# Softmax probabilities normalised on GpSimd instead of on VectorE and ScalarE

## The chip, the cores and the metric

The kernel runs on one core of a Trainium2 chip. The core has a matrix engine (TensorE, in the profile PE, its weight loads PEld), VectorE (DVE), ScalarE (ACT), GpSimd (POOL) and a queue that issues transfers (SyncE, SP). The engines run beside each other, each through its own list of instructions in order, and wait for each other by semaphores. The metric is the device time of one execution in microseconds; the time before is the median of three runs.

## The reference

One inference step of a two-layer trunk for 128 context tokens and 512 latent tokens that share the weights. Every layer projects its normalised input, runs a gated convolution, grouped-query attention and a state-space scan beside each other, adds up the three gated branches, and ends in a SwiGLU. What matters here is attention, for 16 query heads over 4 key heads of 64 channels; a latent block of 128 queries sees 512 latent and 128 cached keys:

```python
s = jnp.einsum('bqkrd,bskd->bkrqs', qi, k).astype(jnp.float32)
p = jax.nn.softmax(s, axis=-1).astype(v.dtype)
return jnp.einsum('bkrqs,bskd->bqkrd', p, v)
```

## The kernel before

All 640 tokens go through a layer together. A matrix product takes its weights and its activations as pairs of high and low halves, three products each, accumulated in PSUM. Weights come in through SP, ACT makes the high half (tile `wh`) and DVE the low half.

Attention works in tiles of 128 queries of one head against 640 keys, 64 such tiles a layer, and after every 16 a smaller one for the context tokens of four heads. A tile goes through these steps, each a generator of its own: `attn_scores` (line 1271) multiplies q by k on PE and takes the row extreme on DVE (into `mx`); `attn_exp` (line 1254) exponentiates on ACT from PSUM into a tile `c` and gets the row sums; `attn_norm` (line 1236) takes the reciprocal of the sums on DVE and multiplies the tile by it, in place; `attn_turn` (line 1308) transposes it on PE by five products with the identity (`bps<-ident,c`); `attn_split` makes a high half (ACT) and a low half (DVE) of the transposed tile, in `pt`; `attn_out` multiplies by V on PE (`bps<-pt,c`) and adds up the result.

The order of the instructions is not written out. A planner in the program does it: it keeps a clock for each engine (class `Clock`), every recorded instruction adds a cost to it (lines 133 to 163; all instructions are recorded at line 132, and so the profile shows that line), and `pump` (line 538) lets the generator step next that can start first by these clocks, as long as that is no later than what the main thread could do. The main thread, `layer` (line 1895), issues the projections: during attention these are the q projections, the gates (`gates`), the GLU of the scan branch and its output branch. Then comes `drain(att)` (line 1946), which steps attention alone until it is finished, and the projection of attention's output after it. In the planner's clock a norm on DVE costs 70 + 640 / 1.6 = 470, one on ACT 100 + 640 / 1.2 = 633; a dependence between engines adds a hop of 100.

Before the change, `attn_norm` picks the engine whose clock is behind (line 1243). POOL issues transfers only: those of the FFN weights that are added to what is in `pt`.

Of the kernel before, what the change touches and what calls it, by code (L numbers as in the profile page):

```python
# [10 lines left out]
AF = mybir.ActivationFunctionType  # L11
OP = mybir.AluOpType
# [100 lines left out]
class Engine:  # L113
# [5 lines left out]
    def __getattr__(self, op):  # L119
        f, key, clock = getattr(self.eng, op), self.key, self.clock  # L120

        def is_ap(x):
            return hasattr(x, "partition_size")

        def size(x):
            n = 1
            for d in x.shape[1:]:
                n *= d
            return n

        def call(*args, **kw):
            res = f(*args, **kw)  # L132
            out = kw.get("out", args[0] if args else None)
            ins = [x for x in list(args[1:] if "out" not in kw else args) +
                   [v for k, v in kw.items() if k not in ("out", "accum_out")] if is_ap(x)]
            outs = [out.name] + ([kw["accum_out"].name] if "accum_out" in kw else [])
            n = max([size(out)] + [size(x) for x in ins]) if key != "pe" else size(out)
            if key == "pe":
                if op == "transpose":
                    cost = 2 * n / 2.4  # L140
                elif ins[-1].dtype == F32R:
                    cost = max(n, 256) / 2.4
                else:
                    cost = 4 * n / 2.4
                    if out.shape[0] == 32:
                        cost /= 3
            elif key == "act":
                cost = 100 + n / 1.2 + (90 if "accum_out" in kw else 0)
            elif key == "dve":
                one = op in ("tensor_scalar", "tensor_copy", "memset") and all(x.space == out.space for x in ins)  # L150
                cost = 70 + n / (1.6 if one else 0.96)
            else:
                s = max([clock.t["pe"] if key == "dma" else clock.t[key]] + [clock.avail.get(x, 0.0) for x in outs] +
                        [clock.w.get(x.name, 0.0) for x in ins])
                if key == "pool":
                    clock.t[key] = e = s + 1000
                else:
                    clock.issue = max(clock.issue, s) + 475.0
                    rate = 180.0 if min(x.shape[-1] for x in [out] + ins) < 128 else 360.0
                    clock.t[key] = e = max(clock.t[key], clock.issue) + 4 * n * out.shape[0] / rate  # L160
                for x in outs:
                    clock.w[x], clock.by[x] = e + (4000 if key == "pool" else 2000), "dma"
                return res
            clock.op(key, cost, outs, [x.name for x in ins])
            return res
        return call
# [3 lines left out]
def trunk_kernel(ctx: ExitStack, tc: tile.TileContext, a):  # L170
    nc = tc.nc
    clk = Clock()
    pe, act, dve, sp, pool = (Engine(e, k, clk) for e, k in (
        (nc.tensor, "pe"), (nc.scalar, "act"), (nc.vector, "dve"), (nc.sync, "dma"), (nc.gpsimd, "pool")))
# [49 lines left out]
    def mul(out, x, y):  # L224
        tt(out, x, y, OP.mult)
# [10 lines left out]
    def ts(out, in0, s1, s2=None, op0=OP.mult, op1=OP.add):  # L236
        if s2 is None:
            dve.tensor_scalar(out=out, in0=in0, scalar1=s1, scalar2=None, op0=op0)
        else:
            dve.tensor_scalar(out=out, in0=in0, scalar1=s1, scalar2=s2, op0=op0, op1=op1)  # L240
# [995 lines left out]
    def attn_norm(exps, probs):  # L1236
        for n in range(4 * 17):
            yield lambda: len(exps) > n
            P, mx = exps[n]
            yield P,  # L1240
            if n % 17 < 16:
                dve.reciprocal(mx[:, 2:3], mx[:, 1:2])
                if clk.t["act"] < clk.t["dve"]:
                    act.activation(P, P, AF.Copy, scale=mx[:, 2:3])
                else:
                    ts(P, P, mx[:, 2:3])
            else:
                dve.reciprocal(mx[:, 8:12], mx[:, 4:8])
                p4 = P[:, 0:512].rearrange("p (h n) -> p h n", h=4)
                mul(p4, p4, mx[:, 8:12][:, :, None].to_broadcast([128, 4, 128]))  # L1250
            probs.append(P)
            exps[n] = None
# [125 lines left out]
    def attn_begin(l, A, raws, ya):  # L1378
        preps, scores, exps, probs, turned, pts, done = [], [], [], [], [], [], [0] * 5
        out = Side(attn_out(preps, pts, done, ya), 0)  # L1380
        Side(attn_split(turned, pts, done), 0.1)
        Side(attn_turn(probs, turned, done), 0.2)
        Side(attn_norm(exps, probs), 0.5)
        Side(attn_exp(scores, exps), 0.7)
        Side(attn_scores(preps, scores, exps, done), 1)
        Side(attn_prep(l, A, raws, preps, done), 2)
        return out
# [785 lines left out]
```

## Time and profile before

| | us |
|---|---|
| median of three runs (2588.91 to 2592.42) | 2589.41 |
| the profiled execution | 2593.81 |
| its span in the trace | 2591.8 |
| PE busy | 2494.3 (96%) |
| DVE busy | 1838.0 (71%) |
| ACT busy | 1155.5 (45%) |
| POOL busy | 97.9 (4%) |

The profile is of one execution, and sums are made against its own time; it lies 4.4 us above the median. Matmuls are pipelined, so PE's busy time says when it had work and not how well it did it. Idle time of an engine matters where that engine is the one that the rest waits for.

### The profile page before, as it was taken

The numbers are of one execution on the slowest core, as the hardware profiler recorded it, in microseconds if no ns is written. First come the engines' busy times: TensorE is split into PE (matmuls) and PEld (weight loads), VectorE is DVE, ScalarE is ACT, GpSimd is POOL, SyncE is SP. The second block draws the span as 40 slices with busy tenths as digits, with TensorE's granted clock in tenths as the row PEclk, the third lists the DMA queues.
The fourth block names the chain that finished last, engine by engine and source line by source line (L and its number), as shares of the span: only waits on it lengthen the run. The fifth ranks groups of instructions, "written<-read, shape, count | busy, mean of one in ns | idle before, by whom it ended". The sixth has DMA issues, their size and how long they took to land. (4 is left out here: it accounts for less than half of the span.)

```text
span 2591.8 us, 45359 instructions
## 1 busy us (share of the span) xinstructions
PE 2494.3 (96%) x18235; PEld 2398.9 (93%) x18235; DVE 1838.0 (71%) x3502; ACT 1155.5 (45%) x2096; POOL 97.9 (4%) x80
## 2 busy tenths in 40 slices
PE   6999999999999999999989999999998999999998
PEld 4899999999888899999979999899997889999998
DVE  5888787788744666675678887777887447766665
ACT  4343336556722533443443333365666225433443
POOL 0000000000000010111000000000000000111110
PEclk8999999999999999999989999999999999999999
DMA  9433331221037366665553233212110572565552
GB/s 267 139 106 114 96 96 51 64 67 42 17 114 237 92 144 141 147 145 128 122 167 94 78 99 117 63 44 86 52 45 24 175 201 58 118 143 123 114 125 72
DMA packets 465202, 280.46 MB, mean 108 GB/s; under 512 B 60184, under 2 KB 453216, under 8 KB 464992
## 3 DMA queue, kind: packets, MB, share of 16 engines
q1 hardware_dynamic: 424864, 257.63, 34.2%
q0 software_dynamic: 40128, 19.93, 6.2%
q8 instruction: 144, 2.36, 0.4%
q14 instruction: 66, 0.54, 0.1%
HBM read 257.37 MB, written 20.12 MB: 107 GB/s over the span
## 5 line engine op out<-in xcount | busy, mean ns | idle before, releaser
L132 PE MATMUL bps<-c,wh 128*128 128x320 f32 x11760 | 1822.7, 313 | 42.0 <-ACT c L132 20.7
L132 PEld LDWEIGHTS bps<-c,wh 128*128 128x128 f32 x11760 | 1745.3, 189 | 77.5 <-ACT c L132 25.8
L132 DVE TENSOR_TENSOR c<-c,c 128x512 f32<-128x512 f32 (+8 forms) x750 | 423.8, 592 | 57.9 <-ACT c L132 47.8
L132 ACT CAST wh<-wr 128x1024 fp32r<-128x1024 f32 (+2 forms) x286 | 267.9, 940 | 315.6 <-PE bps L132 157.7
L132 DVE TENSOR_TENSOR wh<-wr,wh 128x1024 fp32r<-128x1024 f32 (+2 forms) x286 | 309.3, 1086 | 129.7 <-ACT wh L132 128.6
L132 ACT COPY c<-bps 128x320 f32<-128x320 f32 (+7 forms) x363 | 150.7, 437 | 255.5 <-PE bps L132 250.8
L132 PE MATMUL bps<-c,c 128*128 128x320 f32 (+2 forms) x1416 | 234.8, 303 | 10.1 <-DVE c L132 6.5
L132 PEld LDWEIGHTS bps<-c,c 128*128 128x128 f32 x1416 | 204.4, 191 | 15.1 <-ACT c L132 10.4
L132 DVE TENSOR_TENSOR c<-c,bps 128x320 f32<-128x320 f32 (+1 forms) x222 | 125.0, 564 | 122.2 <-ACT c L132 106.4
L132 ACT ACTIVATE c<-c 128x640 f32<-128x640 f32 (+4 forms) x131 | 93.5, 722 | 210.2 <-DVE c L132 210.0
L132 PE MATMUL bps<-wh,c 128*128 128x256 f32 x1440 | 183.7, 286 | 2.9 <-ACT c L132 2.7
L132 PE MATMUL bps<-ident,c 128*128 128x128 f32 (+1 forms) x1115 | 159.2, 279 | 23.8 <-DVE c L132 9.9
L132 PEld LDWEIGHTS bps<-wh,c 128*128 128x128 f32 x1440 | 177.4, 193 | 3.8 <-ACT c L132 3.3
L132 ACT CAST c<-c 128x640 fp32r<-128x640 f32 (+3 forms) x192 | 113.4, 619 | 117.9 <-DVE c L132 116.8
L132 PEld LDWEIGHTS bps<-ident,c 128*128 128x128 f32 (+1 forms) x1115 | 131.1, 144 | 35.9 <-issue 10.2
L132 DVE SCALAR_TENSOR_TENSOR c<-bps,g2T,c 128x128 f32<-128x128 f32 (+2 forms) x240 | 89.7, 433 | 84.6 <-PE bps L132 84.6
L132 POOL DMA_DIRECT2D pt<-in_w_ffn_gate_dram x38 | 48.9, 1287 | 2344.8 <-DMA pt<-in_w_ffn_up_dram 2018.6
L132 DVE SCALAR_TENSOR_TENSOR c<-c,c 128x640 f32<-128x640 f32 (+3 forms) x124 | 102.8, 836 | 47.2 <-ACT c L132 45.4
L132 ACT ACTIVATE c<-bps,mx 128x640 f32<-128x640 f32 (+1 forms) x160 | 113.3, 712 | 36.4 <-DVE mx L132 35.7
L132 DVE TENSOR_REDUCE mx<-bps 128x1 f32<-128x640 f32 (+1 forms) x136 | 109.6, 809 | 27.8 <-PE bps L132 27.2
L132 ACT CAST wh<-pt 128x1024 fp32r<-128x1024 f32 x76 | 79.9, 1051 | 84.9 <-PE bps L132 83.7
L132 DVE TENSOR_TENSOR pt<-bps,pt 128x640 fp32r<-128x640 f32 (+1 forms) x136 | 109.4, 810 | 9.9 <-ACT pt L132 8.9
(105 smaller groups left out, 1541.2 us busy)
## 6 DMA issues: line engine op xcount, KB each, us to landing
wr<-in_w_in_dram SPq DMA_DIRECT2D x104, 512.0 KB
c<-in_w_ada_dram SPq DMA_DIRECT2D x110, 256.0 KB
wr<-in_w_ffn_gate_dram SPq DMA_DIRECT2D x44, 512.0 KB
wr<-in_w_ada_dram SPq DMA_DIRECT2D x41, 512.0 KB
pt<-in_w_ffn_up_dram SPq DMA_DIRECT2D x38, 512.0 KB
wr<-in_w_ffn_down_dram SPq DMA_DIRECT2D x48, 256.0 KB
wr<-in_w_ffn_down_dram SPq DMA_DIRECT2D x32, 320.0 KB
pt<-in_w_ffn_up_dram SPq DMA_DIRECT2D x38, 256.0 KB
```

The source lines that it names most:

```text
L132: res = f(*args, **kw)
```

## The change

The norm of the 128 tiles over 640 elements is issued on POOL (`tensor_scalar` with the reciprocal as a scalar for each row) and no longer on DVE or ACT. The planner's clock gets a cost for such an instruction, 1000, and notes its output as written by POOL. The reciprocal stays on DVE, and so does the whole norm of the eight smaller tiles.

```diff
--- before.py
+++ after.py
@@ -154,6 +154,10 @@
                         [clock.w.get(x.name, 0.0) for x in ins])
                 if key == "pool":
                     clock.t[key] = e = s + 1000
+                    if op != "dma_start":
+                        for x in outs:
+                            clock.w[x], clock.by[x] = e, key
+                        return res
                 else:
                     clock.issue = max(clock.issue, s) + 475.0
                     rate = 180.0 if min(x.shape[-1] for x in [out] + ins) < 128 else 360.0
@@ -1240,10 +1244,7 @@
             yield P,
             if n % 17 < 16:
                 dve.reciprocal(mx[:, 2:3], mx[:, 1:2])
-                if clk.t["act"] < clk.t["dve"]:
-                    act.activation(P, P, AF.Copy, scale=mx[:, 2:3])
-                else:
-                    ts(P, P, mx[:, 2:3])
+                pool.tensor_scalar(out=P, in0=P, scalar1=mx[:, 2:3], scalar2=None, op0=OP.mult)
             else:
                 dve.reciprocal(mx[:, 8:12], mx[:, 4:8])
                 p4 = P[:, 0:512].rearrange("p (h n) -> p h n", h=4)
```

With it the planner's decisions change inside the two attention stretches; ahead of, between and behind them every engine's order is the same.

On DVE, at the beginning of the first layer's attention (`mx` holds a tile's row statistics, `c_4666` is the second tile of probabilities), the norm between two reciprocals goes:

```order
 L132 TENSOR_REDUCE mx<-bps 128x1 x2
 L132 TENSOR_TENSOR c_4641<-c_4071,c_4641 128x5x64
-L132 RECIPROCAL mx<-mx 128x1
-L132 TENSOR_SCALAR c_4666<-c_4666,mx 128x640
-L132 RECIPROCAL mx<-mx 128x1
+L132 RECIPROCAL mx<-mx 128x1 x2
```

Only the reciprocals are left there; the norm of `c_4666` stands on POOL now.

On PE, a little later in the same stretch (`c_4882` is the sixth tile of probabilities, `c_526` and `c_533` are halves of activations with weights in `wh`, `c_4359` and `c_4360` queries, `c_4610` keys), the transposes of a tile move behind other work:

```order
 L132 MATMUL bps<-c_526,wh 128x320 x2
 L132 MATMUL bps<-c_525,wh 128x320 x2
-L132 MATMUL bps<-ident,c_4882 128x128 x5
-L132 MATMUL bps<-c_533,wh 128x320 x2
-L132 MATMUL bps<-c_534,wh 128x320 x2
-L132 MATMUL bps<-c_533,wh 128x320 x2
 L132 MATMUL bps<-c_4359,c_4610 128x320
 L132 MATMUL bps<-c_4360,c_4610 128x320
 L132 MATMUL bps<-c_4359,c_4610 128x320
 L132 MATMUL bps<-c_4360,c_4610 128x320
+L132 MATMUL bps<-c_533,wh 128x320 x2
+L132 MATMUL bps<-c_534,wh 128x320 x2
+L132 MATMUL bps<-c_533,wh 128x320 x2
+L132 MATMUL bps<-ident,c_4882 128x128 x5
```

Six projection matmuls and four of the next tile's scores stand ahead of the transposes now.

On PE, at the end of the second layer's attention, before the change (`c_14170` and `c_14171` are the last activations of the gates, the last projection ahead of the drain; `ident` with a `c` is a tile's transposes):

```order
L132 MATMUL bps<-c_14170,wh 128x320 x2
L132 MATMUL bps<-c_14171,wh 128x320 x2
L132 MATMUL bps<-c_14170,wh 128x320 x2
L132 MATMUL bps<-ident,c_21365 128x128 x5
L132 MATMUL bps<-c_20991,c_21326 128x320
L132 MATMUL bps<-c_20992,c_21326 128x320
```

And with the change, the same place:

```order
L132 MATMUL bps<-c_14170,wh 128x320 x2
L132 MATMUL bps<-c_14171,wh 128x320 x2
L132 MATMUL bps<-c_14170,wh 128x320 x2
L132 MATMUL bps<-ident,c_21516 128x128 x5
L132 MATMUL bps<-ident,c_21525 128x128 x5
L132 MATMUL bps<-pt,c_20916 128x256 x10
L132 MATMUL bps<-c_20895,c_21399 128x320
L132 MATMUL bps<-c_20896,c_21399 128x320
```

Behind the last projection nine tiles of 640 keys are still to be transposed before the change, and four with it; in the first layer eight and six.

On POOL, with the change, the list of the first layer's norms (`c` with its number is a tile of probabilities) ends, and the FFN's transfers follow:

```order
L132 TENSOR_SCALAR c_8053<-c_8053,mx 128x640
L132 TENSOR_SCALAR c_8075<-c_8075,mx 128x640
L132 TENSOR_SCALAR c_8089<-c_8089,mx 128x640
L132 TENSOR_SCALAR c_8109<-c_8109,mx 128x640
L132 DMA pt<-in_w_ffn_gate_dram 128x4x128
L132 DMA pt<-in_w_ffn_up_dram 128x4x128
```

No transfer stands between two norms of one layer. An ISA instruction that loads a library stands ahead of the first norm.

## Rows read from the trace of the kernel before

**Rows 1.** Windows: us, then busy us (instructions) of each engine, clock, DMA.

```profile
0.00:400.00 400.00, 371.28 (x2989) 346.83 (x2990) 318.98 (x726) 153.53 (x315) 0.20 (x4) 0.97 0.47 134
400.00:693.00 293.00, 287.63 (x2067) 281.85 (x2066) 225.99 (x424) 186.32 (x372) 0.00 (x0) 0.98 0.17 51
693.00:717.00 24.00, 18.13 (x118) 15.35 (x116) 18.25 (x37) 17.91 (x41) 0.00 (x0) 0.93 0.00 1
...
1680.00:1967.00 287.00, 283.13 (x2061) 277.90 (x2060) 221.95 (x416) 182.80 (x363) 0.00 (x0) 0.99 0.17 52
1967.00:1995.00 28.00, 21.93 (x153) 18.52 (x151) 22.63 (x46) 20.58 (x47) 0.00 (x0) 1.00 0.00 1
```

**Rows 2.** The tile of statistics: operations, ns min/median/max, first and last start.

```profile
L132 DVE RECIPROCAL mx<-mx x136: 134/156/180, 405.8 to 1989.3; 128x1 f32<-128x1 f32 x128, 128x4 f32<-128x4 f32 x8
L132 DVE TENSOR_SCALAR c<-c,mx x84: 552/553/559, 407.9 to 1987.7; 128x640 f32<-128x640 f32 x84
L132 ACT ACTIVATE c<-c,mx x44: 828/831/835, 406.0 to 1971.6; 128x640 f32<-128x640 f32 x44
```

**Rows 3.** Groups of PE: 400 to 717; transposes 400 to 693, 1680 to 1967 us.

```profile
L132 PE MATMUL bps<-ident,c 128*128 128x128 f32 x429 | 60.5, 275 | 3.7 <-DVE c L132 1.7 <-ACT c L132 1.3 <-DVE mx L132 0.5
L132 PE MATMUL bps<-c,c 128*128 128x320 f32 x256 | 49.9, 317 | 1.9 <-ACT c L132 1.4 <-DVE c L132 0.5
L132 PE MATMUL bps<-pt,c 128*128 128x256 f32 x320 | 45.2, 289 | 0.2 <-DVE pt L132 0.2
...
L132 PE MATMUL bps<-ident,c 128*128 128x128 f32 x388 | 54.1, 274 | 0.3 <-ACT c L132 0.2
...
L132 PE MATMUL bps<-ident,c 128*128 128x128 f32 x370 | 52.6, 274 | 0.8 <-ACT c L132 0.5 <-DVE c L132 0.2
```

**Rows 4.** Timeline, the first and the last tile: start, us, instruction, idle before.

```profile
406.01 0.83 ACT L132 ACTIVATE c<-c,mx 128x640 f32<-128x640 f32 x1 [0.23 <-DVE mx L132]
407.67 0.77 PE L132 MATMUL bps<-ident,c 128*128 128x128 f32 x5
...
1987.66 0.56 DVE L132 TENSOR_SCALAR c<-c,mx 128x640 f32<-128x640 f32 x1
1988.79 0.71 PE L132 MATMUL bps<-ident,c 128*128 128x128 f32 x5
```

**Rows 5.** Groups of DVE: first and last two-tensor kind, 400 to 717; scan, whole.

```profile
L132 DVE TENSOR_TENSOR wh<-wr,wh 128x1024 fp32r<-128x1024 f32 x22 | 26.9, 1222 | 16.0 <-ACT wh L132 15.9
...
L132 DVE TENSOR_TENSOR c<-c,c 128x64 fp32r<-128x64 f32 x6 | 1.1, 219 | 0.0
...
L132 DVE TENSOR_TENSOR_SCAN c<-c,c 64x320 f32<-64x320 f32 x64 | 52.4, 818 | 0.8
```

**Rows 6.** POOL: a group of its memsets, and its first transfer in the timeline.

```profile
L2159 POOL MEMSET const-float32-1.0<- 128x1 f32 x1 | 0.1, 99 | 0.0
...
881.35 1.43 POOL L132 DMA_DIRECT2D pt<-in_w_ffn_gate_dram  x1 [880.91 <-DMA pt<-in_w_ffn_up_dram]
```

**Rows 7.** Timeline of PE: one projection, and from the first layer's drain.

```profile
649.76 1.93 PE L132 MATMUL bps<-c,wh 128*128 128x320 f32 x12
...
696.46 1.61 PE L132 MATMUL bps<-ident,c 128*128 128x128 f32 x10 [0.50 <-DVE mx L132]
...
712.00 1.09 PE L132 MATMUL bps<-ident,c 128*128 128x128 f32 x4 [1.35 <-DVE c L132]
```

**Rows 8.** A gap of the first layer's GLU: PE's timeline, then windows.

```profile
477.12 3.30 PE L132 MATMUL bps<-c,wh 128*128 128x320 f32 x11 [2.77 <-ACT c L132]
...
476.00:480.00 4.00, 2.88 (x11) 2.88 (x12) 3.46 (x5) 3.95 (x7) 0.00 (x0) 0.56 0.00 0
480.00:484.00 4.00, 4.00 (x21) 3.99 (x20) 1.99 (x3) 0.85 (x3) 0.00 (x0) 0.59 0.59 176
```

## The prediction

> **What bounds the kernel now.** I read the windows first [rows 1]. The reader is to see TensorE (PE) busy 98% or more in the two stretches in which attention runs beside projections (400 to 693 us and 1680 to 1967 us), and clearly less in the 24 and 28 us that follow each of them, where attention alone is left: 18.13 and 21.93 us. VectorE (DVE) stands at 77% and ScalarE (ACT) at 64% in the long stretches, GpSimd (POOL) at nothing in all four. So PE is the bound, and what the change can win lies in PE's idle time there: 5.4 + 5.9 + 3.9 + 6.1 = 21 us. Second come the operations on the tile of row statistics [rows 2]: of 128 normalisations, 84 stand on DVE at 0.553 us and 44 on ACT at 0.831 us, a mean of (84 x 0.553 + 44 x 0.831) / 128 = 0.65 us. Third is who waits for a normalised tile: PE transposes it. In the two long stretches its transposes had 0.3 and 0.8 us of idle time before them, in the first layer's whole attention 3.7 us, nearly all of it in the drain [rows 3]. The two places that I show have a gap between the end of the normalisation and the transposes of 407.67 - 406.84 = 0.83 us (the first of the 128 tiles) and 1988.79 - 1988.22 = 0.57 us (the last) [rows 4]. Worked out in this way for all 128 the median gap is 0.84 us; 40 are below 0.4, 60 below 0.8, 98 below 1.5. So the norm is nearly on PE's path: half a microsecond more, with the order unchanged, would be felt.
>
> **What the change removes.** DVE loses 84 x 0.553 = 46.5 us and ACT 44 x 0.831 = 36.6 us, over some 630 us of attention. By themselves these are worth nothing where PE is solid. The reciprocal (0.156 us) stays on DVE, so DVE's queue still decides when a norm can begin. The 8 tiles of the context pass (four heads each) are still normalised on DVE.
>
> **What it adds.** 128 instructions on POOL, each over 128x640 f32 in place with one scalar a row. The trace has no arithmetic on POOL. From below, the same instruction on DVE takes 0.553 us [rows 2]. From above, the slowest arithmetic per element in this trace is DVE's scan, 0.818 us for 320 elements [rows 5], which makes 1.64 us for 640. The nearest row is ACT's norm, 0.831 us for the same work one element at a time; POOL's own fixed cost shows as 0.1 us in a memset of one element [rows 6]. I take 0.83 + 0.1 and round to 1.0 us, and keep 0.55 and 1.64 for the range. For POOL as a queue this is nothing: 64 us of work a layer in 317 us. Nothing else stands in it: its first DMA is issued at 881 us [rows 6], and in the new order all 64 norms of a layer stand ahead of the FFN's DMAs. The one ISA instruction that appears ahead of POOL's first norm has 400 us in which POOL does nothing [rows 1].
>
> In the Trainium skill (GPSIMD Engine Reference, section 3.1) a two-input add of 2048 f32 takes 4497 ns on GpSimd against 2293 ns on VectorE. Scaled to 640 elements that is an estimate of 1.4 us, inside my range; no run here shows it, and by it the third term below would grow by at most 10 x 0.4 = 4 us, and the sum be -3 us.
>
> **What the change moves.** The planner writes every engine's order by its own clock, and that clock now charges a norm 1000 instead of 470 (DVE) or 633 (ACT), with a hop of 100 before it. So it puts the transposes later. Counted in the order over the 128 tiles, 51.8 matmuls stand on average between a tile's last score product and its first transpose, and 44.5 before; at the lowest tenth 31.7 and 26. PE takes 1.93 us for 12 of the common ones [rows 7], 0.16 us each, so PE has 7.3 x 0.16 = 1.17 us (lowest tenth 0.9 us) more of other work to do before it asks for the tile. POOL at 1.0 us plus some 0.1 us of signalling needs 1.1 - 0.65 = 0.45 us more than now. The cover is larger than the delay: I expect the waits of transposes in the long stretches not to grow.
>
> The other move is at the end of each layer's attention. Before, 8 tiles (first layer) and 9 (second) are still to be transposed after the last projection matmul; in the new order 6 and 4. These are the tiles that PE handles with nothing else to do.
>
> **The sum.** Term one, the drains: a tile costs 24 / 8 = 3.0 us and 28 / 9 = 3.1 us of the drain, and 2.2 us of PE time (49.9 / 64 for scores, 60.5 x 5 / 429 for transposes, 45.2 / 64 for the product with V; [rows 3]). Two tiles leave one drain and five the other: 2 x 0.8 + 5 x 0.9 = 6.1 us. From below: the drain's fixed head and tail do not shrink with its tiles. Between the transposes at 696.46 and those at 712.00 lie seven tiles at 2.2 us [rows 7], just the PE time, and by that the gain is near nothing; from above, the drains cannot give back more than PE's idle time in them, 5.9 + 6.1 = 12 us [rows 1]. Between them I take 6, since the windows are the rows that hold the whole drain. Term two, transposes that wait in the long stretches: the 0.3 and 0.8 us [rows 3] may go; I take 1 us, bounds 0 and 1.1. Term three, the ten tiles left in the drains: there nothing covers POOL, 10 x 0.45 us = 4.5 us at worst; but DVE and ACT, busy 76 to 81% and 74% there [rows 1], are each freed of their share (0.65 us a tile). I set it at 0. The sum is -7 us: the profiled execution goes from 2593.8 us (span 2591.8) to 2586.8. The median of the runs is 2589.4, 4.4 us under the profiled one, and so I predict 2582.4, as a round number 2582 us. The rest of the program has the same order on every engine outside the two attention stretches.
>
> **Rivals.**
> 1. POOL is too slow, and the kernel gets slower. A norm meets a DVE instruction that it cannot run beside, and the two take turns. In the first layer's 317 us, DVE works 78.8 us (25%) on the 12 kinds of instruction that read two SBUF tensors, the weights' low halves above all [rows 5]; one of these takes up to 1.22 us. With 1.64 us for the work and 0.6 for half of such an instruction in front of it, the norm needs 2.3 us with signalling, 1.65 more than now and 0.5 more than the cover. The gaps below 0.5 us fall short by 13 us in sum; a stall gives the next tile time, so I count two thirds, 9 us; the ten drain tiles add 10 x (1.65 - 0.65) = 10 us; less the 6 us of term one that is +13 us, some 2602 us. It decides from 0.65 + 1.17 = 1.8 us on. Against it: with 1.0 us the same meeting costs 25% x 0.6 = 0.15 us on average, and DVE has 46.5 us less to do. The Trainium skill (SBUF — State Buffer, section "Who interferes with whom") has this as a rule: VectorE with two SBUF inputs and a GpSimd instruction that reads SBUF share one read interface, and the later one blocks for the whole of the other. No row here shows POOL and DVE at such a meeting.
> 2. The drain is latency, not work: it keeps its length, and only the 1 us of term two is won, with some of term three against it. Then 2587 to 2591, no change. For it speaks the 2.2 us a tile in the middle of the drain, and that the reciprocal, which stays in DVE's queue, holds the norm as before.
> 3. More is won. The two gaps of the GLU in the first layer (PE waits 2.77 us at 477, and its granted clock is 0.56 and 0.59 in the 8 us around, close to the lower of its two levels, 1.2 of 2.4 GHz [rows 8]) shrink when DVE and ACT have fewer norms queued before the GLU's splits. 2 us of wait and 8 x (1 - 0.575) = 3.4 us of slow clock for the one gap make 5 to 6 us on top of the forecast, and the time is 2577. Against it: the chain at that gap is the GLU's own split, ACT and DVE by turns, with no norm in it.
>
> **Chances.** Forecast (2578.5 to 2584) 0.38; rival 3, 0.15; rival 2, 0.27; rival 1, 0.20. A measurement of this kernel tells about 0.2%, 5.2 us, from no change. Faster by more than that: 0.38 + 0.15 = 0.53; within: 0.27; slower: 0.20. The range, 2573 to 2598, leaves out the far half of rival 1 and the far third of rival 3. The likeliest case's own range is 2578.5 to 2584.
>
> **What the new profile would show.** POOL busy some 64 us in each attention stretch with about 1.0 us a norm; no DVE or ACT norm over 640 elements; DVE's two-tensor instructions as long as now (wh at 1.22 us); PE's drains some 18 to 20 and 13 to 15 us long with 6 and 4 tiles. The prediction is wrong if a norm takes over 1.6 us from its reciprocal to its end, if PE's waits for transposes grow in the long stretches, or if the drains keep 24 and 28 us with fewer tiles in them.

## The result, and the profile after

The changed kernel takes 2612.68 us (median of 5 runs, 2612.29 to 2616.66) against 2589.41 before in the same comparison: a ratio of 1.0087, 95% interval 1.0076 to 1.0098, 23 us slower. The prediction said 2582 and 2573 to 2598. The profiled execution took 2612.3 us, with a span of 2610.5; that is 18.7 more than the span before.

First the windows, as in [rows 1], cut where the last projection matmul of each attention stretch ends now (us, then busy us and instructions of PE, PEld, DVE, ACT, POOL, then clock and DMA):

```profile
400.00:703.60 303.60, 289.89 (x2085) 279.05 (x2083) 216.81 (x394) 175.38 (x357) 111.83 (x59) 1.00 0.16 49
703.60:723.00 19.40, 14.06 (x102) 12.14 (x101) 12.84 (x26) 13.60 (x33) 9.67 (x6) 1.00 0.01 1
1682.00:1995.70 313.70, 299.52 (x2169) 289.54 (x2167) 219.88 (x402) 180.99 (x371) 116.01 (x61) 1.00 0.16 48
1995.70:2012.00 16.30, 11.03 (x70) 9.20 (x70) 9.35 (x19) 9.64 (x24) 5.67 (x4) 0.90 0.00 1
```

Subtract PE's busy time in each row: PE idles 13.7 and 14.2 us in the long stretches, where it was 5.4 and 3.9, and 5.3 and 5.3 us in the drains, where it was 5.9 and 6.1 [rows 1]. The sum is 38.5 against 21.2, so 17 of the 18.7 us are new idle time of PE in attention: 18.6 more in the long stretches, 1.3 less in the drains. (The medians lie 23 us apart, since the profiled execution of before lay 4.4 us above its median.) PE's busy time over the whole program did not change (2494.3 and 2493.8 us). POOL works 121.5 and 121.7 us in the two layers' attention, not 64.

The operations on the tile of statistics say why (ns minimum/median/maximum), the answer to [rows 2]:

```profile
L132 DVE RECIPROCAL mx<-mx x136: 138/158/180, 406.2 to 2005.5; 128x1 f32<-128x1 f32 x128, 128x4 f32<-128x4 f32 x8
L132 POOL TENSOR_SCALAR c<-c,mx x128: 1872/1884/2377, 406.5 to 2003.1; 128x640 f32<-128x640 f32 x128
```

A norm takes 1.88 us on POOL, 3.4 times DVE's 0.553. It is also steady, so this is the instruction's own length. Who waits is shown by the transposes, as in [rows 3]; the four rows are the four windows above in their order:

```profile
L132 PE MATMUL bps<-ident,c 128*128 128x128 f32 x395 | 57.2, 276 | 6.8 <-POOL c L132 6.0 <-DVE c L132 0.5
...
L132 PE MATMUL bps<-ident,c 128*128 128x128 f32 x34 | 5.2, 282 | 4.0 <-POOL c L132 3.0 <-DVE mx L132 0.8 <-DVE c L132 0.2
...
L132 PE MATMUL bps<-ident,c 128*128 128x128 f32 x405 | 58.0, 276 | 10.6 <-POOL c L132 9.2 <-DVE pt L132 1.1
...
L132 PE MATMUL bps<-ident,c 128*128 128x128 f32 x24 | 3.7, 285 | 4.0 <-POOL c L132 3.1 <-ACT pt L132 0.8
```

In the long stretches they had 0.3 and 0.8 us of idle time before them [rows 3]; now it is 6.8 and 10.6, and "<-POOL c" ended nearly all of it. One such wait in the timeline of the second layer (start, us, engine, in brackets the idle time before):

```profile
1783.15 0.16 DVE L132 RECIPROCAL mx<-mx 128x1 f32<-128x1 f32 x1
1783.18 1.04 PE L132 MATMUL bps<-c,wh 128*128 128x320 f32 x6
...
1783.47 1.88 POOL L132 TENSOR_SCALAR c<-c,mx 128x640 f32<-128x640 f32 x1 [26.10 <-PE bps L132]
1785.41 0.77 PE L132 MATMUL bps<-ident,c 128*128 128x128 f32 x5 [1.18 <-POOL c L132]
```

The norm starts 0.16 us after its reciprocal's end and ends at 1785.35. PE's other work runs out at about 1784.2, and its transposes start 0.06 us after the norm's end. The first and the last tile, which answer to [rows 4], look the same:

```profile
406.53 7.47 POOL L132 TENSOR_SCALAR c<-c,mx 128x640 f32<-128x640 f32 x4 [406.10 <-DVE mx L132]
...
408.47 0.77 PE L132 MATMUL bps<-ident,c 128*128 128x128 f32 x5 [0.33 <-POOL c L132]
...
2003.08 1.88 POOL L132 TENSOR_SCALAR c<-c,mx 128x640 f32<-128x640 f32 x1 [2.70 <-DVE mx L132]
2005.02 0.77 PE L132 MATMUL bps<-ident,c 128*128 128x128 f32 x5 [1.77 <-POOL c L132]
```

The first row also shows a queue: four norms end to end, 7.47 us. Worked out for all 128 tiles, 42 norms stand behind the one before them, and the mean from a reciprocal's end to its norm's end is 0.47 + 1.91 = 2.37 us; before it was 0.04 + 0.65 = 0.69. Transposes that start within 0.2 us of the norm, and so had waited for it, are 55 of 128, and were 29.

### The profile page after: what moved, and what is told of

It is laid out like the page before. It is cut to its first block, busy times and chain, and to the rows that moved or that the text cites. A ratio compares the mean times of both kernels' runs of the same rounds, so it can differ in the third digit from the quotient of the medians.

```text
span 2610.5 us, 45661 instructions
## 1 busy us (share of the span) xinstructions
PE 2493.8 (96%) x18235; PEld 2391.8 (92%) x18235; DVE 1807.3 (69%) x3418; ACT 1125.2 (43%) x2052; POOL 341.1 (13%) x208
## 5 line engine op out<-in xcount | busy, mean ns | idle before, releaser
L132 DVE TENSOR_TENSOR c<-c,c 128x512 f32<-128x512 f32 (+7 forms) x750 | 429.8, 600 | 55.8 <-ACT c L132 45.8
L132 POOL TENSOR_SCALAR c<-c,mx 128x640 f32<-128x640 f32 x128 | 243.2, 1906 | 1224.2 <-DVE mx L132 1151.7
```

## The experiments

Each was timed beside the kernel before, whose medians there were 2591 to 2593 us; so the ratios (95% interval in brackets) are what to compare. The cover of a tile is the work that PE's order puts between the tile's last score product and its first transpose. Two theories run through the experiments: the time is lost because that cover is shorter than what POOL needs (theory A in e1, e3, e9, e10 and e11), or because POOL and DVE hold each other up at SBUF (theory B in e1, e3, e4 and e6). Elsewhere the letters stand for what the expectation says.

**e1: the planner is told the true cost.**

```diff
-                    clock.t[key] = e = s + 1000
+                    clock.t[key] = e = s + (1000 if op == "dma_start" else 1950)
```

> The normalisation stays on GpSimd as in the changed kernel; only the planner's clock is told 1950 for it instead of 1000, near the 1.88 us that the trace of the changed kernel shows. In the new order 59.5 matmuls stand on average between a tile's last score product and its first transpose (51.8 in the changed kernel), 41 at the lowest tenth (31.7), and 4 and 4 tiles are left for the drains (6 and 4). Theory A (the time is lost because GpSimd's 1.88 us was not covered by the order, PE waits): the lowest tenth gains 9 x 0.16 = 1.5 us of cover, most of the 19 us that PE idles more ahead of the transposes goes, and the time is 2586 to 2594. Theory B (VectorE and GpSimd hold each other up at SBUF, whatever the order): it stays at 2608 to 2614. Theory C (the new order itself, with its later transposes, is what costs): it gets slower still, 2615 or more.

Measured: 2591.65 us, ratio 0.9996 [0.9987, 1.0005]. The whole loss is gone, with every norm still on POOL at 1.89 us. That is theory A. The windows of e1, cut as above:

```profile
400.00:699.80 299.80, 290.51 (x2104) 285.06 (x2103) 218.75 (x400) 177.02 (x361) 115.23 (x60) 0.99 0.16 49
699.80:713.00 13.20, 9.80 (x73) 8.45 (x72) 9.08 (x19) 10.13 (x26) 7.48 (x4) 1.00 0.01 2
...
1672.00:1974.50 302.50, 296.25 (x2164) 290.63 (x2163) 220.87 (x401) 179.19 (x368) 114.60 (x60) 0.99 0.17 50
1974.50:1988.00 13.50, 10.10 (x75) 8.73 (x73) 9.34 (x20) 10.40 (x26) 7.48 (x4) 1.00 0.00 1
```

With POOL at work as long as in the changed kernel, PE idles 9.3 + 3.4 + 6.3 + 3.4 = 22.4 us, level with before. The reader is to see the drains too: half as long as before (13.2 and 13.5 us for 24 and 28 [rows 1]), with 5.2 us less idle time between them than 12.0, and nothing won, since the long stretches idle 15.6 us for 9.3. The waits have moved to other matmuls: over the whole program PE idles 50.4 us ahead of the projections (`bps<-c,wh`), 42.0 before.

**e2: the changed order, the norm on VectorE and ScalarE.** Engines that charge the planner's clock as POOL does, but issue on DVE and ACT:

```diff
+    vp, ap_ = Engine(nc.vector, "pool", clk), Engine(nc.scalar, "pool", clk)
...
-                pool.tensor_scalar(out=P, in0=P, scalar1=mx[:, 2:3], scalar2=None, op0=OP.mult)
+                if n % 17 % 3 == 2:
+                    ap_.activation(P, P, AF.Copy, scale=mx[:, 2:3])
+                else:
+                    vp.tensor_scalar(out=P, in0=P, scalar1=mx[:, 2:3], scalar2=None, op0=OP.mult)
```

> PE's order is that of the changed kernel, instruction for instruction, but the normalisation runs on VectorE (two tiles in three) and ScalarE (one in three) as before; the planner's clock still charges it as a GpSimd instruction of 1000. Theory A: the order alone brings what the prediction's first two terms said, -6 and -1, so 2580 to 2586. Theory B: the order is neutral, 2587 to 2592. Theory C (the order costs by itself): 2600 to 2612.

Measured: 2609.16 us, 1.0060 [1.0047, 1.0074]. It fits theory C of this list by its number, but not by its reason: e4 below has the same order of PE and is level with before. Nor do the transposes wait for the norm here: 4 of 128 start within 0.2 us of it, 55 in the changed kernel. e13 below differs from e2 by these 128 norms alone and is 20 us faster. So a fast norm that the planner has not entered in the queues of DVE and ACT costs 20 us here, not much less than the slow one on POOL (27 by the same count). Half of it is seen in the traces: PE waits 10 us longer than in e13 for tiles that DVE and ACT make (37.2 against 34.3 us for `c` of DVE, 35.8 against 32.2 for `c` of ACT, 6.5 against 2.8 for `pt` of DVE). The other half, PE's busy time (2499.7 us against 2487.4), stays open. The run does not show what I wanted of it, the worth of the order by itself; e13 does.

**e3: the old order, the norm on POOL.**

```diff
+    pa, pd = Engine(nc.gpsimd, "act", clk), Engine(nc.gpsimd, "dve", clk)
...
+                eng = pa if clk.t["act"] < clk.t["dve"] else pd
+                eng.tensor_scalar(out=P, in0=P, scalar1=mx[:, 2:3], scalar2=None, op0=OP.mult)
```

> The order of PE is that of the kernel before, instruction for instruction; the planner charges the normalisation to VectorE or ScalarE as before, but GpSimd executes it. Theory A: 1.7 us more from reciprocal to end of the norm against gaps with a median of 0.84 us; the shortfalls of 102 of the 128 tiles sum to 108 us, and of these two thirds count, since a stall gives the next tile time: some +70 us, 2640 to 2670, far above the changed kernel. Theory B (hold-ups at SBUF alone): the same GpSimd work as in the changed kernel, so 2608 to 2616. Theory C: the order of before is the better one, so under 2612.

Measured: 2663.72 us, 1.0267 [1.0247, 1.0286], some +70 us, as theory A had it. The transposes' group of the whole program, before, in the changed kernel, in e1 and then in e3:

```profile
L132 PE MATMUL bps<-ident,c 128*128 128x128 f32 (+1 forms) x1115 | 159.2, 279 | 23.8 <-DVE c L132 9.9
```

```profile
L132 PE MATMUL bps<-ident,c 128*128 128x128 f32 (+1 forms) x1115 | 162.8, 281 | 39.5 <-POOL c L132 21.4
```

```profile
L132 PE MATMUL bps<-ident,c 128*128 128x128 f32 (+1 forms) x1115 | 159.7, 279 | 19.3 <-DVE c L132 6.3
```

```profile
L132 PE MATMUL bps<-ident,c 128*128 128x128 f32 (+1 forms) x1115 | 167.4, 286 | 76.6 <-POOL c L132 58.2
```

The same instruction on the same engine costs 70, 23 or 0 us, by the order that surrounds it.

**e4 and e9: a shorter instruction in the changed order.** Only the first 320 (e9: 480) columns are multiplied:

```diff
-                pool.tensor_scalar(out=P, in0=P, scalar1=mx[:, 2:3], scalar2=None, op0=OP.mult)
+                pool.tensor_scalar(out=P[:, 0:320], in0=P[:, 0:320], scalar1=mx[:, 2:3], scalar2=None, op0=OP.mult)
```

> The changed kernel with the order unchanged on every engine, but GpSimd multiplies only the first 320 of the 640 columns of each tile; the other 320 stay unnormalised. Theory A: one instruction takes 0.95 to 1.05 us, the duration that the prediction took, and the time is what its sum gave for it, 2580 to 2588. Theory B (hold-ups in proportion to GpSimd's busy time): half of the loss goes, about 2600. Theory C (order or signalling): 2608 to 2613.

> As e4 (the order of the changed kernel, unchanged on every engine), with GpSimd multiplying the first 480 of the 640 columns; the other 160 stay unnormalised. From e4's 1.09 us for 320 columns and the changed kernel's 1.88 us for 640 it should take about 1.49 us. Theory A (the order covers a norm up to some length, and beyond it PE waits): with 0.3 us of queue and signalling the norm ends 1.8 us after its reciprocal, just the point that the prediction's first rival named, so a small loss, 2594 to 2602. Rival (each 0.1 us costs the same, no threshold): halfway between e4 (no difference) and the changed kernel (+23), 2602 to 2606.

Measured: e4 2593.20 us, 0.9998 [0.9987, 1.0009]; e9 2598.44 us, 1.0029 [1.0016, 1.0041]. The instruction, in e4 and in e9:

```profile
L132 POOL TENSOR_SCALAR c<-c,mx x128: 1076/1087/1585, 405.6 to 1979.1; 128x320 f32<-128x320 f32 x128
```

```profile
L132 POOL TENSOR_SCALAR c<-c,mx x128: 1475/1485/1979, 405.5 to 1992.3; 128x480 f32<-128x480 f32 x128
```

From reciprocal to norm's end the means are 1.32, 1.82 and 2.37 us (e4, e9, changed kernel), and the losses 0, 7 and 23 us: the longer the norm, the dearer each further 0.1 us. There is no sharp point: against e13 below, the same order without the norm, which lies 4 us under before, even e4's 1.09 us cost some 4 (barely clear of the noise), the next 0.4 us cost 8, and the last 0.4 cost 15. Transposes within 0.2 us of their norm are 13, 39 and 55 of 128, so tiles run out of cover one after another. e9 came as its theory A said; e4's theory A had expected 2580 to 2588, the prediction's gain, and there is none. POOL's time is 0.29 us and 2.49 ns an element by these three sizes.

**e6: POOL's work with nobody waiting for it,** in the kernel before:

```diff
+    dum = const.tile([128, 256], F32, name="dum")
+    nc.gpsimd.memset(dum, 1.0)
...
+                for _ in range(2):
+                    nc.gpsimd.tensor_scalar(out=dum, in0=dum, scalar1=mx[:, 2:3], scalar2=None, op0=OP.mult)
```

> The kernel before, with GpSimd work that nobody waits for: after each of the 128 norms, GpSimd multiplies a tile of its own of 128x256 twice by the same reciprocals, some 2 x 0.93 = 1.86 us, as long as its norm in the changed kernel, and at the same places. PE's, VectorE's and ScalarE's order is that of before. It measures by itself what GpSimd's work does to the others. Theory A: a few VectorE instructions with two SBUF inputs get 0.2 to 0.3 us longer (some 30 to 40 of them, 10 us of VectorE's time at most, which mostly idles anyhow): 2589 to 2597. Theory B (hold-ups at SBUF are the loss): 2605 to 2615.

Measured: 2594.61 us, 1.0009 [1.0000, 1.0018], 2 us of 23. Theory B falls as the cause, here as in e1. A meeting is there all the same; POOL's instructions by length, in e6:

```profile
L1250 POOL TENSOR_SCALAR dum<-dum,mx x256: 922/926/2162, 406.0 to 1987.2; 128x256 f32<-128x256 f32 x128
```

and one meeting in its timeline:

```profile
1873.19 2.83 POOL L1250 TENSOR_SCALAR dum<-dum,mx 128x256 f32<-128x256 f32 x2
1874.00 1.23 DVE L132 TENSOR_TENSOR wh<-wr,wh 128x1024 fp32r<-128x1024 f32 x1 [1.16 <-ACT wh L132]
```

These two instructions of POOL take 2.83 us instead of 2 x 0.92: the second, from 1874.2 on, is some 0.9 us longer than usual, while `wh`, begun 0.2 us earlier, runs at its usual 1.23 us. The Trainium skill (SBUF — State Buffer, "Who interferes with whom") calls the port pair that the two engines share an exclusive lock, and says that the order of issue decides who blocks. This meeting agrees: the later one is longer by 0.9 us, and `wh` still had 1.0 us to run. What all the meetings cost the kernel is the 2 us.

**e10 and e11: other costs in the planner,** 1450 and 2400 in e1's line.

> The normalisation on GpSimd, charged 1450 in the planner's clock (1000 in the changed kernel, 1950 in e1). 52.5 matmuls of cover on average, 36 at the lowest tenth (31.7 and 41), 7 and 7 tiles in the drains. Theory A (the loss is the part of 1.88 us that the order doesn't know of): 0.43 us is missing instead of 0.88, so half or less of the 23 us is lost, 2596 to 2604. Rival (e1 came out level by the luck of one order, since orders alone have moved the time by 0 to 10 us): no trend, 2605 to 2615.

> The normalisation on GpSimd, charged 2400: more than it takes. 67.2 matmuls of cover on average, 46.7 at the lowest tenth, 4 and 2 tiles in the drains. Theory A: once the wait for GpSimd is covered, more cover wins nothing, and the idle time that leaves the drains comes back as waits ahead of other matmuls: 2588 to 2596. Rival (fewer tiles in the drains do win, as the prediction's first term said): 2580 to 2586.

Measured: e10 2608.05 us, 1.0064 [1.0051, 1.0077]; e11 2592.59 us, 1.0002 [0.9993, 1.0011]. The transposes' group in e10 and in e11:

```profile
L132 PE MATMUL bps<-ident,c 128*128 128x128 f32 (+1 forms) x1115 | 162.6, 281 | 29.2 <-POOL c L132 12.6
```

```profile
L132 PE MATMUL bps<-ident,c 128*128 128x128 f32 (+1 forms) x1115 | 159.6, 279 | 23.8 <-DVE c L132 10.5
```

Charged 1000, 1450, 1950 and 2400, the loss is 23, 17, 0 and 0 us. e10 missed my 2596 to 2604 and lies in its rival's range (no trend). I take it that I counted the cost and not the cover: 52.5 matmuls on average are hardly more than the 51.8 of the changed kernel, against 59.5 and 67.2. At 0.16 us each, the 8 more than before are 1.3 us of cover, for a norm that ends 1.8 us later (2.52 us after its reciprocal against 0.69), so a loss was due; why the order came out so is open. Nor is e1 the luck of one order: two orders with the full cost are level, and PE's waits for POOL over the whole program (us, times, longest) go with the losses. They are, in the changed kernel, e10, e1 and e11 (loss 23, 17, 0, 0 us), then in e4, e9 and e3 (0, 7, 70 us):

```profile
PE bps L132 <- POOL c L132: 21.4, 37, 1.8
PE bps L132 <- POOL c L132: 12.6, 28, 1.2
PE bps L132 <- POOL c L132: 2.6, 4, 1.1
PE bps L132 <- POOL c L132: 2.8, 3, 1.8
...
PE bps L132 <- POOL c L132: 3.4, 7, 1.0
PE bps L132 <- POOL c L132: 7.5, 13, 1.4
PE bps L132 <- POOL c L132: 58.2, 66, 2.0
```

e11 has the fewest tiles in the drains, 4 and 2, and wins nothing by it.

**e5, e7, e8: three other orders.** In e5 the kernel before takes a normalised tile as ready later; e7 gives each tile to the engine that is done first by the planner's clock; e8 is e1 with the last 8 of 68 tiles on DVE or ACT.

```diff
+                clk.w[P.name] += 450
```

```diff
+                end = dict(act=clk.t["act"] + 633, dve=clk.t["dve"] + 470, pool=clk.t["pool"] + 1950)
+                best = min(end, key=end.get)
```

```diff
+                if n < 60:
+                    pool.tensor_scalar(out=P, in0=P, scalar1=mx[:, 2:3], scalar2=None, op0=OP.mult)
```

> The kernel before, normalisation on VectorE and ScalarE and charged to them in the planner's clock, with one line more: the planner takes the normalised tile as ready 450 later. 48.1 matmuls stand between a tile's last score product and its first transpose (44.5 before); 11 and 8 tiles are left for the drains (8 and 9). It stands beside e2, whose later order ran the same norms without having them in the planner's times of VectorE and ScalarE, and took 2609 us. Theory A (e2 was slow because its 128 norms stood unplanned in the queues of VectorE and ScalarE): here they are planned, so 2586 to 2595. Theory B (transposes put later cost by themselves): 2600 to 2610. Theory C (the prediction's second term, waits of transposes that go, is worth something alone): 2580 to 2586.

> GpSimd as a third engine for the norm, not the only one: the planner takes for each tile whichever of ScalarE (633), VectorE (470) and GpSimd (1950) its clock says will be done first. 54.3 matmuls of cover on average, 8 and 6 tiles left for the drains. Theory A: no wait for GpSimd, and VectorE and ScalarE are relieved of some tiles, but PE is the bound with 21 us idle: 2583 to 2592. A version that beats both would have to come under 2584. Rival: three queues make more late tiles, 2592 to 2605.

> The normalisation on GpSimd charged 1950, as in e1, but for the last 8 of the 68 tiles of each layer, which VectorE or ScalarE normalises as before. 59.2 matmuls of cover, 4 and 4 tiles in the drains. Theory A: in the drains nothing covers GpSimd's 1.88 us, four tiles each wait about 1.2 us less in a layer, of which half counts: e1 less 2 x 2.4 us, 2584 to 2589. Rival: the drain's chain is the last tile's alone, 1.2 us in a layer, 2588 to 2591, no difference from e1 or from before.

Measured: e5 2597.87 us, 1.0025 [1.0014, 1.0037]; e7 2601.09 us, 1.0041 [1.0027, 1.0055]; e8 2595.91 us, 1.0020 [1.0011, 1.0029]. Each is slower than before, and lies 3 to 9 us above the range of its theory A; e7 falls into its rival's range, e5 and e8 into none. Of the 16 us that e2 lost, e5, which enters the norms in the queues, loses 6; where these and those of e7 and e8 come from stays open. PE waits 1.0 us for POOL in e7 and not at all in e8, so it isn't the wait that the changed kernel has. The three say how far one order of this planner lies from another, and that a difference of 10 us between two orders needs no cause in the norm.

**e12 and e13: no norm at all,** in the old and in the changed order. The planner's clock is charged, nothing is issued:

```diff
+class Nop:
+    def __getattr__(self, op):
+        return lambda *args, **kw: None
...
+    na, nd = Engine(Nop(), "act", clk), Engine(Nop(), "dve", clk)
```

> The kernel before without the 128 normalisations of 128x640 (the reciprocals stay, nothing multiplies by them); the planner still charges them to VectorE and ScalarE, so every engine's order is that of before. No engine can take the norm over and do better than this in that order. Theory A (PE is the bound and nearly nothing in its 21 us of idle time hangs on the norm): 2584 to 2591. Rival (the prediction's terms: waits of transposes and drains hang on the norm): 2574 to 2583.

> The changed kernel without its 128 GpSimd instructions; every other engine's order is that of the changed kernel. Theory A (the changed order wins nothing by itself, as e4 said): 2584 to 2592, level with the run that leaves the norm out of the order of before. Rival (the shorter drains are worth 6 us, and e4's 1.09 us hid it): 6 us or more under that run, 2570 to 2580.

Measured: e12 2586.95 us, 0.9976 [0.9967, 0.9985]; e13 2587.60 us, 0.9983 [0.9975, 0.9992]. Both came as their theory A said. Taking the norm away for nothing wins 6 us in the old order (4 to 9 by the interval), and the changed order is no better. The windows of e13, cut as above:

```profile
400.00:694.70 294.70, 287.16 (x2090) 280.28 (x2089) 211.89 (x394) 174.79 (x358) 0.00 (x0) 1.00 0.17 51
694.70:711.80 17.10, 13.64 (x102) 11.90 (x99) 12.66 (x26) 13.39 (x33) 0.00 (x0) 1.00 0.01 1
1670.00:1972.10 302.10, 297.04 (x2183) 291.80 (x2182) 215.69 (x403) 181.45 (x373) 0.00 (x0) 1.00 0.17 51
1972.10:1985.20 13.10, 8.77 (x69) 7.77 (x67) 8.96 (x18) 9.28 (x24) 0.00 (x0) 1.00 0.00 0
```

7.5 + 3.5 + 5.1 + 4.3 = 20.4 us of PE's idle time stay, of 21.2, although nothing is left to wait for between the exponential and the transposes: this idle time does not belong to the norm. Nor do the profiles place the 6 us: PE idles 96.8 us in e12, 98.3 in e13 and 97.5 before (span less busy time), and its busy time, which differs (2487.2, 2487.4 and 2494.3 us), is no higher in e4 (2487.0) and e1 (2485.2), which are level with before.

## Why the prediction was wrong

**The price of POOL's instruction, the step that turned no change into a loss.** "I take 0.83 + 0.1 and round to 1.0 us, and keep 0.55 and 1.64 for the range." It is 1.88 us, above the upper bound too. The bounds came from other engines and the fixed cost from a memset of one element; neither says what POOL needs, which is 0.29 us and 2.49 ns an element. The Trainium skill (GPSIMD Engine Reference, section 3.1), through the price of a two-input add, gave an estimate of 1.4 us that I set beside the sum: nearer, and still short.

**The cover.** "The cover is larger than the delay": the order had the 7.3 matmuls more, 1.17 us as I counted, but the delay is 1.68 us (2.37 against 0.69), not 0.45, since a slower instruction also stands longer behind its own kind. This comparison was the right one to make: it held in e3 (+70 expected, +70 measured), in e4 (0.63 us of delay) and in e1. As a comparison of means it is coarse: e9's delay, 1.13 us, lies just under 1.17, and 7 us are lost, since many tiles have less cover than the mean. Two of my signs of being wrong came: a norm takes over 1.6 us from its reciprocal to its end (2.37), and PE's waits for transposes grew in the long stretches.

**Terms one and two, the gain.** "Two tiles leave one drain and five the other: 2 x 0.8 + 5 x 0.9 = 6.1 us." The drains did shrink, to 19 and 16 us (I had said 18 to 20 and 13 to 15). In e1 they shrink to 13. But a tile that leaves the drain takes its PE work into the long stretch, and idle time appears there for what the drain gives up: 12.0 to 6.8 us in e1's drains, 9.3 to 15.6 in its long stretches. e4 ran the changed order with an instruction of 1.09 us, about the length I had assumed, and was level with before. With that term the prediction would have missed even at its own price: its second rival (no change) was the answer there. e12 shows that the forecast 7 us would have needed a norm that costs nothing: 6 us (4 to 9) is all there is then in the old order, and 4 us (2 to 6) in the changed one.

**Rival 1** had the sign, and 1.8 us as its point of decision: e9 at 1.82 loses 7 us, so losses begin lower. Its mechanism was wrong: it needed meetings with DVE to get from 1.64 to 2.3 us. The instruction takes 1.88 us undisturbed and 1.91 on average, so meetings add 0.02 us to it, and the rest of the 2.37 is signalling and the queue of its own kind (e6: 2 us for all meetings). Its price, 2602, was too low by 11 us: the long stretches idle 18.6 us more (15.2 of it in waits for POOL), where it had 9; the drains went the other way, 1.3 us less idle, where it had 10 - 6 = 4 us more; and 4.4 us are the distance of the profiled execution from the median.

**Term three** was set at 0; in the drains PE waits 3.0 + 3.1 us for POOL. **Rival 3** asked for a shorter GLU gap: it went from 2.77 [rows 8] to 2.23 us,

```profile
479.40 2.02 PE L132 MATMUL bps<-c,wh 128*128 128x320 f32 x12 [2.23 <-ACT c L132]
```

and the granted clock of the 8 us around it is 1.00 now (last column but two), for 0.56 and 0.59:

```profile
476.00:480.00 4.00, 1.77 (x13) 1.51 (x12) 3.14 (x4) 1.98 (x3) 0.00 (x0) 1.00 0.00 0
480.00:484.00 4.00, 4.00 (x30) 3.99 (x29) 3.99 (x8) 3.95 (x10) 0.00 (x0) 1.00 0.26 82
```

It came about in part, and is too small to show in the sum. Its reason was not the one that I gave: the gap is 2.83 us in e12, where DVE and ACT have no norm at all in the old order, and 2.21 us in e2, where they have all of them in the changed order. So the order shortened it, not the relief. The clock is not as firm: 0.62 in 480 to 484 us of e2, which has the same order of PE.

## What to carry to other kernels

Where an order is written by a cost table, the entry for the new instruction is part of the change: the same 1.88 us cost 70 us in an order that knew nothing of it, 23 us at half its price and nothing at its full price. Before crediting a relieved engine, ask what the time would be if the work vanished altogether; here that ceiling was 6 us in the order of before, and idle time taken out of one stretch came back in the next. An operation that no row shows on its engine needs a wider range than its kin on other engines give, or a measurement first.

## What I had not expected of the hardware

POOL needs 3.4 times as long as DVE for a multiplication of one f32 tensor by a scalar per row (1.884 us against 0.553 for 128x640), and its time is a straight line over 256, 320, 480 and 640 columns: 0.92, 1.09, 1.49, 1.88 us. The Trainium skill (GPSIMD Engine Reference, section 4.1) calls operations with one input "roughly line-rate"; the runs here do not agree. When POOL and DVE do meet, either may pay: POOL in the row of e6 above, DVE in the changed kernel, where its 12 additions of 128x512 between 400 and 693 us average 811 ns and not 688 (687 in e13, the same order without the norms). The group, and one such meeting:

```profile
L132 DVE TENSOR_TENSOR c<-c,c 128x512 f32<-128x512 f32 x12 | 9.7, 811 | 0.2
...
450.72 1.89 DVE L132 TENSOR_TENSOR c<-c,c 128x512 f32<-128x512 f32 x2
450.91 2.25 POOL L132 TENSOR_SCALAR c<-c,mx 128x640 f32<-128x640 f32 x1 [8.59 <-DVE mx L132]
```

Both are longer here (two additions take 1.4 us alone, a norm 1.88), and the second addition, which began during the norm, ended 0.55 us before it. So this meeting does not agree with a lock that is held for a whole instruction, as far as the profile's spans on POOL, which are rough, can tell.
